# Attention of two heads at a time on the two row halves of TensorE, with one 512-column score product per head

## Chip, cores and metric

One NeuronCore of one Trainium2 chip runs a whole network of four layers on 512 tokens in one launch. The metric is the device time of that launch in microseconds: the median of three runs, beside one profiled execution from which all rows below come.

## The reference, cut to what matters

The last layer's mixer is a neighbourhood attention with 16 heads of 64 channels. The 512 latent tokens lie on a grid of 8 rows by 64 columns; a token sees, in all 8 rows, 16 columns around its own, and 256 context tokens beside them. One softmax runs over both kinds of keys:

```python
s_loc = jnp.einsum('bhrqd,bhrikd->bhrqik', qg, kg).astype(jnp.float32) * scale + bias
s_loc = jnp.where(col_mask[:, None, :], s_loc, NEG_INF)
s_ctx = jnp.einsum('bhrqd,bhcd->bhrqc', qg, k_c).astype(jnp.float32) * scale
s = jnp.concatenate([s_loc.reshape(B_, H, rows, GRID_W, n_loc), s_ctx], axis=-1)
p = jax.nn.softmax(s, axis=-1).astype(v.dtype)
o = jnp.einsum('bhrqik,bhrikd->bhrqd', p_loc, vg) + jnp.einsum('bhrqc,bhcd->bhrqd', p_ctx, v_c)
```

Queries and keys are normalised per head before (`rms_norm_2` with a gain), and the heads' outputs go through `odd_w_o` afterwards. All of it is float32.

## The kernel before, in words

Activations are kept with channels on the 128 partitions and tokens along the free dimension; a number is split in a high and a low part (float32r), and one exact product is three matmuls, high by high, high by low and low by high (`mm3`, L294 to L298). A tile framework puts the instructions of each engine in an order at build time, by priority (which is the order of the program, with some work raised) and by the readiness that its own cost estimates give; on the chip each engine's queue then runs in that order. `load_w` loads a 512 KB weight tile on the SyncE queue, casts its high part on ScalarE and subtracts the low part on VectorE, well ahead of use.

In `odd` the tokens are sorted by grid column, so that 128 queries (16 grid columns, `j` = 0 to 3) need 256 neighbouring keys from `STARTS[j]`. Two heads share one tile of 128 channels: head `hh` = 0 on partitions 0 to 63, `hh` = 1 on 64 to 127. For each pair of heads `hp_` there is a query tile and a key tile `kx` of 704 columns (512 keys and the first 192 again, for the queries at the edge); the context keys are in tiles `kc` of their own. There are 8 x 4 x 2 = 64 items of one head and 128 queries. An item (`item`, L1591) does:

- scores: `mm3` for 256 grid keys and `mm3` for 256 context keys, contraction over 64 rows, into one PSUM tile (L1598, L1599, in the trace under L296 to L298);
- softmax: bias and mask are added and the maximum of the grid half taken in one VectorE instruction (L1602), the maximum of the context half in another (L1604), their joint maximum negated (L1605), two exponentials with sums on ScalarE (L1607, L1608), the sums added, inverted and multiplied in (L1609 to L1611);
- `turn`: four transposes of 128x128 into PSUM (L1617) and a copy to SBUF on ScalarE (L1619);
- `weigh`: four matmuls with the values, whose 64 output rows are the head's half of a PSUM tile `po` (L1625). The two heads of a pair take turns, one key block each.

The loop issues the scores of an item, then a filling piece of other work (`fill`), then the transposes of the item two before and, once more than five items are in the queue, the weighted sums of the two oldest. The filling comes from `side_steps`: the query and key projections of the following pairs of heads, by pieces of two weight blocks (six matmuls of 512 columns), their head norms (`headnorm`, L1426, with one product against `bd64` at L1432), and at the end the first output projections. `fill` stops at a given piece for the last items so that some is left to the end.

Six PSUM tiles (`mm_ps`) serve scores, transposes, projections and head norms alike; two more (`aux_ps`) hold `po`. Ten SBUF tiles (`tmp`) are shared the same way. The bias of a head is loaded per pair (`tb`, L1669) and added to three masks on GpSimd (L1674), with two slots per mask type. Before the loop, the four slots of the probabilities `pr` hold extra key columns `ex` that only the values' products read.

## Time and profile before

| | |
|---|---|
| runs (three) | 2959.49, 2962.75, 2965.26 us; median 2962.75 |
| profiled execution | 2960.36 us, span from first to last instruction 2958.6 us |
| TensorE matmul, busy share | 97% (weight load 82%) |
| VectorE, ScalarE, GpSimd, busy share | 66%, 39%, 21% |
| granted TensorE clock, mean | 0.992 |
| attention loop | about 2317.7 to 2554.1 us of the span |

Busy shares are sums of the instructions' times. Matmuls are pipelined and their printed times overlap, so a matmul's cost in the queue is the distance from its start to the next one's start. "Idle before, releaser" says how long an engine stood before an instruction and which engine ended it. The TensorE instructions of `mm3` all stand under L296 to L298, and are told apart by their tiles: `kh`, `kl`, `kch`, `kcl` with `qh`, `ql` are scores, `hh`, `hl` with `whi`, `wlo` projections.

### The profile page before, as it was taken

The numbers are of one execution on the slowest core, as the hardware profiler recorded it, in microseconds if no ns is written. First come the engines' busy times: TensorE is split into PE (matmuls) and PEld (weight loads), VectorE is DVE, ScalarE is ACT, GpSimd is POOL, SyncE is SP. The second block draws the span as 40 slices with busy tenths as digits, with TensorE's granted clock in tenths as the row PEclk, the third lists the DMA queues.
The fourth block names the chain that finished last, engine by engine and source line by source line (L and its number), as shares of the span: only waits on it lengthen the run. The fifth ranks groups of instructions, "written<-read, shape, count | busy, mean of one in ns | idle before, by whom it ended". The sixth has DMA issues, their size and how long they took to land.

```text
span 2958.6 us, 41163 instructions
## 1 busy us (share of the span) xinstructions
PE 2867.9 (97%) x15892; PEld 2418.0 (82%) x15892; DVE 1960.5 (66%) x3750; ACT 1159.6 (39%) x1993; POOL 614.5 (21%) x568
## 2 busy tenths in 40 slices
PE   5999999999988999999999999999999999999999
PEld 4888888878877887887888888888888777788887
DVE  8767767987877578898636787633366667662333
ACT  4433344323753432323433422222246677542332
POOL 4000003444223113332102122211101122022220
PEclk9999999999999999999999999999999999999999
DMA  7445433665656435554122345412133211133232
GB/s 268 139 154 167 163 108 114 233 211 176 218 191 207 134 114 172 175 182 135 57 77 93 100 135 189 153 62 68 58 97 119 71 47 44 53 98 96 90 106 72
DMA packets 118004, 380.62 MB, mean 129 GB/s; under 512 B 12720, under 2 KB 22576, under 8 KB 116784
## 3 DMA queue, kind: packets, MB, share of 16 engines
q1 hardware_dynamic: 92464, 285.70, 29.6%
q0 software_dynamic: 25344, 92.29, 9.6%
q8 instruction: 125, 2.05, 0.3%
q14 instruction: 71, 0.58, 0.1%
HBM read 354.87 MB, written 23.07 MB: 128 GB/s over the span
## 4 chain that ended last, share of the span: by engine, by line
PE 57%; DVE 8%; ACT 2%; issue 1%; POOL 0%; ACTq 0%; DVEq 0%; POOLq 0%
PE mm L296 18%; PE mm L297 17%; PE mm L298 17%; PE aux L1625 1%; DVE wlo L291 1%; DVE al L280 1%; DVE aout L583 1%; PE mm L1617 1%; DVE araw L583 1%; DVE t L618 1%; ACT whi L290 1%; PE mm L1432 1%; DVE hl L434 0%; ACT ah L279 0%; DVE t L527 0%
## 5 line engine op out<-in xcount | busy, mean ns | idle before, releaser
L296 PE MATMUL mm<-hh,whi 128*128 128x512 f32 (+1 forms) x2872 | 1040.5, 365 | 12.6 <-ACT whi L290 6.0
L297 PE MATMUL mm<-hl,whi 128*128 128x512 f32 (+1 forms) x2872 | 1034.5, 361 | 16.0 <-POOL hl L426 13.6
L298 PE MATMUL mm<-hh,wlo 128*128 128x512 f32 (+1 forms) x2872 | 1033.0, 360 | 0.6 <-DVE wlo L291 0.5
L290 ACT CAST whi<-raw 128x1024 fp32r<-128x1024 f32 (+3 forms) x448 | 447.1, 1002 | 869.4 <-PE mm L297 735.3
L296 PEld LDWEIGHTS mm<-hh,whi 128*128 128x128 f32 x2872 | 543.3, 190 | 102.8 <-ACT whi L290 6.4
L297 PEld LDWEIGHTS mm<-hl,whi 128*128 128x128 f32 x2872 | 546.0, 190 | 98.6 <-POOL hl L426 15.7
L298 PEld LDWEIGHTS mm<-hh,wlo 128*128 128x128 f32 x2872 | 545.7, 190 | 81.7 <-DVE wlo L291 1.3
L291 DVE TENSOR_TENSOR wlo<-raw,whi 128x1024 fp32r<-128x1024 f32 (+4 forms) x316 | 373.4, 1184 | 210.8 <-ACT whi L290 204.5
L291 POOL TENSOR_TENSOR wlo<-raw,whi 128x1024 fp32r<-128x1024 f32 (+3 forms) x132 | 309.6, 2346 | 920.3 <-ACT whi L290 769.9
L297 PE MATMUL mm<-al,whi 128*128 128x512 f32 (+1 forms) x898 | 330.0, 367 | 3.6 <-DVE al L280 3.6
L296 PE MATMUL mm<-ah,whi 128*128 128x512 f32 (+1 forms) x898 | 329.3, 367 | 2.6 <-ACT ah L279 2.6
L298 PE MATMUL mm<-ah,wlo 128*128 128x512 f32 (+1 forms) x898 | 328.9, 366 | 0.0
L583 DVE CUSTOM_DVE_ANT_0 araw<-araw,cond 128x1024 f32<-128x1024 f32 x192 | 249.3, 1299 | 11.3 <-DMA araw<-in_ada 10.8
L618 DVE SCALAR_TENSOR_TENSOR t<-mm,pk,t 128x511 f32<-128x511 f32 (+5 forms) x286 | 161.1, 582 | 134.2 <-ACT t L620 130.8
L579 POOL DMA_DIRECT2D araw<-in_ada x176 | 96.4, 548 | 657.7 <-DVE mod L583 265.5
L297 PEld LDWEIGHTS mm<-al,whi 128*128 128x128 f32 x898 | 170.6, 190 | 31.3 <-DVE al L280 4.6
L296 PEld LDWEIGHTS mm<-ah,whi 128*128 128x128 f32 x898 | 170.6, 190 | 30.4 <-ACT ah L279 3.0
L298 PEld LDWEIGHTS mm<-ah,wlo 128*128 128x128 f32 x898 | 170.5, 190 | 27.3
L710 DVE SCALAR_TENSOR_TENSOR x<-mm,mod,x 128x512 f32<-128x512 f32 (+1 forms) x115 | 84.3, 734 | 141.3 <-PE mm L298 141.1
L643 DVE TENSOR_TENSOR t<-mm,t 128x512 f32<-128x512 f32 x110 | 70.0, 637 | 150.5 <-PE mm L298 112.2
L642 ACT ACTIVATE t<-t 128x512 f32<-128x512 f32 x110 | 64.6, 588 | 268.1 <-DVE t L618 249.6
L280 DVE TENSOR_TENSOR al<-t,ah 128x512 fp32r<-128x512 f32 x110 | 121.8, 1108 | 41.5 <-ACT ah L279 41.3
(368 smaller groups left out, 3619.2 us busy)
## 6 DMA issues: line engine op xcount, KB each, us to landing
araw<-in_ada POOLq DMA_DIRECT2D x176, 512.0 KB, 4.2
raw<-in_up SPq DMA_DIRECT2D x176, 512.0 KB, 3.5
raw<-in_dn SPq DMA_DIRECT2D x32, 448.0 KB, 3.3
raw<-in_dn SPq DMA_DIRECT2D x32, 384.0 KB, 3.1
raw<-in_qk SPq DMA_DIRECT2D x24, 512.0 KB, 3.5
raw<-in_dn SPq DMA_DIRECT2D x32, 320.0 KB, 2.9
araw<-in_ada SPq DMA_DIRECT2D x16, 512.0 KB, 4.6
raw<-in_rqk SPq DMA_DIRECT2D x16, 512.0 KB, 4.4
```

The source lines that it names most:

```text
L280: eng.tensor_tensor(lo, full, hi.bitcast(F32), ALU.subtract)
L290: S.copy(hi[:, :n], raw[:, :n])
L291: next(W["low"]).tensor_tensor(lo[:, :n], raw[:, :n], hi[:, :n].bitcast(F32), ALU.subtract)
L296: T.matmul(o, lhsT=lh[0], rhs=rh[0], start=first, stop=False)
L297: T.matmul(o, lhsT=lh[0], rhs=rh[1], start=False, stop=False)
L298: T.matmul(o, lhsT=lh[1], rhs=rh[0], start=False, stop=last)
L579: (nc.sync if l == 0 and f < 16 else G).dma_start(raw, a[f"ada{l}"][f])
L583: tc.keep_in_program_order(V.tensor_tensor_reduce(out=o, in0=raw, in1=A[c], scale=1.0, scalar=0.0, op0=ALU.mult, op1=ALU.add, accum_out=m))
L618: V.scalar_tensor_tensor(to, fr, cw[q], to, ALU.mult, ALU.add)
L642: S.activation(t, t, AF.Silu)
L643: V.tensor_mul(t, pv, t)
L710: V.scalar_tensor_tensor(xv, p, gates[st.tag][:, f:f + 1], xv, ALU.mult, ALU.add)
```

## The change

The loop goes by pairs of heads, 32 steps instead of 64 items. Context keys are copied by GpSimd behind the grid keys of `kx` (960 columns instead of 704), and a score product takes 256 grid keys and 256 context keys in one matmul of 512 columns with a two-part access pattern. The two heads' matmuls alternate, row half 0 and row half 1, each head into its own PSUM tile: six matmuls a pair instead of twelve. One VectorE instruction per head adds the bias, which is zero over the context columns, negates, and takes the minimum over all 512; one exponential per head with scale -1 follows, then the reciprocal and the scaling. The probabilities now live in the shared `tmp` tiles. A step issues the scores of this pair, the weighted sums of two steps ago, a filling piece, the transposes of the step before, and another filling piece. Bias tiles are allocated once, 512 columns wide; their left half is loaded by DMA and masked in place when the type's last reader of the pair has been issued, so each bias is loaded three times per head. The extra key columns `ex` lie in the slots of two bias types.

```diff
--- before.py
+++ after.py
@@ -1503,7 +1503,7 @@
             V.tensor_scalar(qg, par("qg"), 0.125, None, ALU.mult)
             np2 = stk.enter_context(pool("na2", 2))
             qk = {}
-            ex = [np2.tile([P, 512], F32, tag="pr", name=nm("ex"), bufs=4).bitcast(F32R) for _ in range(4)]
+            ex = [np2.tile([P, 512], F32, tag=f"b{ty}", name=nm("ex")).bitcast(F32R) for ty in (0, 0, 2, 2)]
 
             def ext(k):
                 e = [ex[k // 2][:, (2 * (k % 2) + i) * P:(2 * (k % 2) + i + 1) * P] for i in range(2)]
@@ -1531,14 +1531,17 @@
                     elif step == 9:
                         take(hq, 1)
                     elif step == 15:
-                        kx = (np2.tile([P, 704], F32R, tag="kh", name=nm("kh")), np2.tile([P, 704], F32R, tag="kl", name=nm("kl")))
+                        kx = (np2.tile([P, 960], F32R, tag="kh", name=nm("kh")), np2.tile([P, 960], F32R, tag="kl", name=nm("kl")))
                         hk = headnorm(p, L, par("kg"), kx[0][:, :L], kx[1][:, :L])
+
+                        for i in range(2):
+                            G.tensor_copy(kx[i][:, 704:], kc[hp_][i].bitcast(F32))
                         next(hk)
                     if k % 2:
                         yield
                 take(hk, 1)
-                S.copy(kx[0][:, L:], kx[0][:, :192].bitcast(F32))
-                V.tensor_copy(kx[1][:, L:], kx[1][:, :192].bitcast(F32))
+                S.copy(kx[0][:, L:704], kx[0][:, :192].bitcast(F32))
+                V.tensor_copy(kx[1][:, L:704], kx[1][:, :192].bitcast(F32))
                 qk[hp_] = (q, kx)
 
             os_ = [None] * KT
@@ -1588,51 +1591,58 @@
                 then.h = os_
                 by_halves(then, (5, 6, 7), last_tile, last_add, True)
 
-            def item(hd, j, bias, po):
-                hp_, hh = divmod(hd, 2)
-                rows = slice(64 * hh, 64 * hh + 64)
+            def scores(hp_, j):
+
                 s0 = STARTS[j]
                 q, kx = qk[hp_]
-                p = mm_ps()
-                qs = (q[0][rows, j * P:(j + 1) * P], q[1][rows, j * P:(j + 1) * P])
-                mm3(p[:, :256], qs, (kx[0][rows, s0:s0 + 256], kx[1][rows, s0:s0 + 256]), True, True)
-                mm3(p[:, 256:], qs, (kc[hp_][0][rows, :], kc[hp_][1][rows, :]), True, True)
-                s_ = tmp(256)
-                m = small(4)
-                V.tensor_tensor_reduce(out=s_, in0=p[:, :256], in1=bias[(1, 0, 0, 2)[j]], scale=1.0,
-                                       scalar=NEG, op0=ALU.add, op1=ALU.max, accum_out=m[:, 0:1])
-                V.tensor_reduce(m[:, 1:2], p[:, 256:], mybir.AxisListType.X, ALU.max)
-                V.tensor_scalar(m[:, 0:1], m[:, 0:1], m[:, 1:2], -1.0, ALU.max, ALU.mult)
-                pr = np2.tile([P, 512], F32, tag="pr", name=nm("pr"), bufs=4)
-                S.activation(pr[:, :256], s_, AF.Exp, bias=m[:, 0:1], scale=1.0, accum_out=m[:, 2:3])
-                S.activation(pr[:, 256:], p[:, 256:], AF.Exp, bias=m[:, 0:1], scale=1.0, accum_out=m[:, 3:4])
-                V.tensor_add(m[:, 2:3], m[:, 2:3], m[:, 3:4])
-                V.reciprocal(m[:, 2:3], m[:, 2:3])
-                V.tensor_scalar(pr, pr, m[:, 2:3], None, ALU.mult)
-                pt, prT = [], []
-
-                def turn():
-                    pt.append(mm_ps())
+                ps_ = [mm_ps(), mm_ps()]
+                for qi, ki in ((0, 0), (0, 1), (1, 0)):
+                    for hh in range(2):
+                        rows = slice(64 * hh, 64 * hh + 64)
+                        k_ = kx[ki][rows, s0:s0 + 512]
+                        k_ = dataclasses.replace(k_, ap=[k_.ap[0], [704 - s0, 2], [1, 256]])
+                        T.matmul(ps_[hh].rearrange("p (a b) -> p a b", a=2), lhsT=q[qi][rows, j * P:(j + 1) * P], rhs=k_,
+                                 start=(qi, ki) == (0, 0), stop=qi == 1)
+                prs = []
+                for hh in range(2):
+                    pr = tmp()
+                    m = small(3)
+
+                    V.tensor_tensor_reduce(out=pr, in0=ps_[hh], in1=bias[(1, 0, 0, 2)[j]][hh], scale=-1.0,
+                                           scalar=-NEG, op0=ALU.add, op1=ALU.min, accum_out=m[:, 0:1])
+                    S.activation(pr, pr, AF.Exp, bias=m[:, 0:1], scale=-1.0, accum_out=m[:, 1:2])
+                    V.reciprocal(m[:, 2:3], m[:, 1:2])
+                    V.tensor_scalar(pr, pr, m[:, 2:3], None, ALU.mult)
+                    prs.append(pr)
+                return prs
+
+            def turned(prs):
+                res = []
+                for pr in prs:
+                    p = mm_ps()
                     for b in range(4):
-                        T.transpose(pt[0][:, b * P:(b + 1) * P], pr[:, b * P:(b + 1) * P], ident)
-                    prT.append(tmp())
-                    S.copy(prT[0], pt[0])
-
-                def weigh():
-                    keys = [vt[j][:, hd * 64:(hd + 1) * 64], vt[(j + 1) % 4][:, hd * 64:(hd + 1) * 64]]
-                    keys += [vc[i][hd // 4][:, (hd % 4) * 64:(hd % 4) * 64 + 64] for i in range(2)]
-                    for b in range(4):
-                        T.matmul(po[rows, j * P:(j + 1) * P], lhsT=keys[b],
-                                 rhs=prT[0][:, b * P:(b + 1) * P], start=(b == 0), stop=(b == 3))
-                        yield
-                    if hh == 1 and j == 3:
-                        o = [cpool.tile([P, LC], F32R, tag=f"h{i}c{hp_}", name=nm("o")).bitcast(F32) for i in "hl"]
-                        for i in range(2):
-                            S.copy(o[i], po[:, i * LC:(i + 1) * LC])
-                        ot.append(o)
-                        if hp_ >= 6:
-                            join(hp_)
-                return turn, weigh
+                        T.transpose(p[:, b * P:(b + 1) * P], pr[:, b * P:(b + 1) * P], ident)
+                    res.append(tmp())
+                    S.copy(res[-1], p)
+                return res
+
+            def weigh(hp_, j, prT, po):
+                keys = []
+                for hd in (2 * hp_, 2 * hp_ + 1):
+                    at = slice((hd % 4) * 64, (hd % 4) * 64 + 64)
+                    keys.append([vt[j][:, hd * 64:(hd + 1) * 64], vt[(j + 1) % 4][:, hd * 64:(hd + 1) * 64]]
+                                + [vc[i][hd // 4][:, at] for i in range(2)])
+                for b in range(4):
+                    for hh in range(2):
+                        T.matmul(po[64 * hh:64 * hh + 64, j * P:(j + 1) * P], lhsT=keys[hh][b],
+                                 rhs=prT[hh][:, b * P:(b + 1) * P], start=(b == 0), stop=(b == 3))
+                if j == 3:
+                    o = [cpool.tile([P, LC], F32R, tag=f"h{i}c{hp_}", name=nm("o")).bitcast(F32) for i in "hl"]
+                    for i in range(2):
+                        S.copy(o[i], po[:, i * LC:(i + 1) * LC])
+                    ot.append(o)
+                    if hp_ >= 6:
+                        join(hp_)
 
             ot = []
             side = side_steps()
@@ -1647,51 +1657,39 @@
                     done[0] += 1
                     take(side, 1)
 
-            queue = []
-
-            def advance(t, w):
-
-                n = len(queue)
-                if n > t and not queue[n - 1 - t][2]:
-                    queue[n - 1 - t][0]()
-                    queue[n - 1 - t][2] = True
-                if n > w:
-                    heads = [queue.pop(0)[1]() for _ in range(2)]
-                    for _ in range(5):
-                        for g in heads:
-                            take(g, 1)
-
-            po = None
-            for hp_ in range(8):
-                bias, tb = [{}, {}], []
+
+            bias = [[np2.tile([P, 512], F32, tag=f"b{ty}", name=nm("b")) for _ in range(2)] for ty in range(3)]
+            for ty in range(3):
                 for hh in range(2):
-                    tb_ = np2.tile([P, 256], F32, tag="tb", name=nm("tb"))
-                    nc.sync.dma_start(tb_, a["rpb"][2 * hp_ + hh])
-                    tb.append(tb_)
-                for ty in (1, 0, 2):
-                    for hh in range(2):
-                        b = np2.tile([P, 256], F32, tag=f"b{ty}", name=nm("b"))
-                        G.tensor_tensor(b, tb[hh], msk[:, ty, :], ALU.add)
-                        bias[hh][ty] = b
-                po = aux_ps()
-                for j in range(4):
-                    for hh in range(2):
-                        queue.append([*item(2 * hp_ + hh, j, bias[hh], po), False])
-
-                        fill(72 if hp_ == 7 and j > 1 else 67)
-                        advance(2, 5)
-            while queue:
-                fill(72)
-                for e in queue:
-                    if not e[2]:
-                        e[0]()
-                        e[2] = True
-                        break
-                if queue[1][2]:
-                    heads = [queue.pop(0)[1]() for _ in range(2)]
-                    for _ in range(5):
-                        for g in heads:
-                            take(g, 1)
+                    G.memset(bias[ty][hh][:, 256:], 0.0)
+
+            def biases(hp_, ty):
+                for hh in range(2):
+                    b = bias[ty][hh][:, :256]
+                    nc.sync.dma_start(b, a["rpb"][2 * hp_ + hh])
+                    G.tensor_tensor(b, b, msk[:, ty, :], ALU.add)
+
+            for ty in (1, 0, 2):
+                biases(0, ty)
+            steps = [(hp_, j) for hp_ in range(8) for j in range(4)]
+            prs, prT, pos = {}, {}, {}
+            for n in range(len(steps) + 2):
+
+                upto = 72 if n > 29 else 67
+                if n < len(steps):
+                    hp_, j = steps[n]
+                    if j == 0:
+                        pos[hp_] = aux_ps()
+                    prs[n] = scores(hp_, j)
+                    if hp_ < 7 and j != 1:
+                        biases(hp_ + 1, (1, None, 0, 2)[j])
+                if n > 1:
+                    hp_, j = steps[n - 2]
+                    weigh(hp_, j, prT.pop(n - 2), pos[hp_])
+                fill(upto)
+                if 0 < n <= len(steps):
+                    prT[n - 1] = turned(prs.pop(n - 1))
+                fill(upto)
             take(side, 100)
 
     def dump(name):
```

## Rows read from the trace of the kernel before

**Rows 1.** The loop: us; busy of PE, PEld, DVE, ACT, POOL; clock, DMA share.
```profile
2317.65:2554.10 236.45, 235.64 (x1556) 180.58 (x1555) 162.63 (x540) 162.59 (x441) 50.94 (x56) 1.00 0.13 41
```

**Rows 2.** Chain that ended last, 2326 to 2502 us, by line.
```profile
by line: PE mm L296 29.0%; PE mm L298 19.0%; PE mm L297 18.9%; PE aux L1625 14.6%; PE mm L1617 12.0%; PE mm L1432 6.5%; issue 0.0%
```

**Rows 3.** Waits of PE in the loop: total us, times, longest.
```profile
PE aux L1625 <- ACT t L1619: 0.4, 1, 0.4
PE mm L1432 <- DVE sm L1605: 0.3, 1, 0.3
```

**Rows 4.** PE in order of time, one pair of heads: start, us, instruction.
```profile
2337.66 0.38 PE L296 MATMUL mm<-kh,qh 64*128 64x256 f32 x1
2337.88 0.28 PE L297 MATMUL mm<-kl,qh 64*128 64x256 f32 x1
...
2338.35 0.27 PE L298 MATMUL mm<-kch,ql 64*128 64x256 f32 x1
2338.55 0.50 PE L296 MATMUL mm<-hh,whi 128*128 128x512 f32 x1
2338.89 0.40 PE L297 MATMUL mm<-hl,whi 128*128 128x512 f32 x1
2339.12 0.39 PE L298 MATMUL mm<-hh,wlo 128*128 128x512 f32 x1
...
2340.05 0.60 PE L1617 MATMUL mm<-ident,pr 128*128 128x128 f32 x4
2340.57 0.38 PE L296 MATMUL mm<-kh,qh 64*128 64x256 f32 x1
...
2341.48 0.50 PE L296 MATMUL mm<-hh,whi 128*128 128x512 f32 x1
...
2343.50 0.66 PE L1625 MATMUL aux<-t,vt 128*64 128x128 f32 x8
...
2344.53 0.38 PE L296 MATMUL mm<-kh,qh 64*128 64x256 f32 x1
```

**Rows 5.** PE in order of time elsewhere: one column group, then four in turn.
```profile
525.25 1.95 PE L990 MATMUL aux<-cm,pad 128*32 128x64 f32 x32 [0.46 <-DVE hl L280]
...
864.03 1.08 PE L1083 MATMUL mm<-u,ident 128*32 128x128 f32 x32 [0.79 <-ACT u L1073]
```

**Rows 6.** Groups by line and shape in the loop (L583: page): busy, mean ns.
```profile
L1602 DVE CUSTOM_DVE_ANT_0 t<-mm,b 128x256 f32<-128x256 f32 x64 | 27.1, 423 | 22.0 <-PE mm L298 21.8
L1602 DVE DVE_READ_ACCUMULATOR2_ANT sm<- 128x1 f32 x64 | 5.3, 83 | 0.0
L1604 DVE TENSOR_REDUCE sm<-mm 128x1 f32<-128x256 f32 x64 | 26.8, 419 | 0.0
L1605 DVE TENSOR_SCALAR sm<-sm 128x1 f32<-128x1 f32 x64 | 13.6, 212 | 0.9
L1609 DVE TENSOR_TENSOR sm<-sm 128x1 f32<-128x1 f32 x64 | 11.6, 182 | 19.3 <-ACT pr L1608 19.0
L1607 ACT ACTIVATE pr<-t,sm 128x256 f32<-128x256 f32 x64 | 32.5, 507 | 13.5 <-DVE sm L1605 13.4
L1607 ACT ACTIVATION_READ_ACCUMULATOR pr<-t,sm 128x1 f32 x64 | 12.1, 189 | 0.0
L1608 ACT ACTIVATE pr<-mm,sm 128x256 f32<-128x256 f32 x64 | 29.4, 459 | 0.0
L1619 ACT COPY t<-mm 128x512 f32<-128x512 f32 x64 | 37.1, 581 | 24.8 <-PE mm L1617 24.8
L583 DVE CUSTOM_DVE_ANT_0 araw<-araw,cond 128x1024 f32<-128x1024 f32 x192 | 249.3, 1299 | 11.3 <-DMA araw<-in_ada 10.8
```

**Rows 7.** Order of time, head norm of a key tile: PE, then DVE.
```profile
2389.99 1.13 PE L1432 MATMUL mm<-t,bd 128*128 128x512 f32 x2
...
2394.83 0.74 DVE L1439 SCALAR_TENSOR_TENSOR t<-mm,pk,t 128x512 f32<-128x512 f32 x1
...
2400.41 0.26 DVE L1541 CAST kl<-kl 128x192 fp32r<-128x192 f32 x1 [1.57 <-POOL kl L1442]
```

## Prediction

> **What bounds the kernel now.** I read the busy shares first, then the chain, then the waits, and only then the order of single instructions. Over the attention loop (first score product to last weighted sum, 236.45 us) TensorE is busy 235.64 us, VectorE and ScalarE 162.6 each, GpSimd 50.9, and the granted clock is 1.00 [rows 1]. That share alone could mislead, as matmul times overlap; so the chain: from 2326 to 2502 us every piece of it lies on TensorE, none on a wait [rows 2]. The waits agree: in the whole loop TensorE waited 0.7 us for other engines, twice [rows 3]. So time taken from TensorE's queue here is time taken from the run, until another engine or a latency comes to the surface.
>
> What that queue does is read from start to start, not from the printed times [rows 4]. One head's scores S take 2337.66 to 2338.55, 0.89 us, for six products of 256 columns on 64 rows; the next item's 40.57 to 41.48 is like it, so 0.90. Inside, neighbours start 0.12 apart (37.88 to 38.35 is four starts), so six would take 0.70, and 0.20 is the edge between full-array and half-array products. A second edge follows: the first full product keeps the queue 0.34 (38.55 to 38.89) where the others take 0.23, so 0.11. The filling piece F of six full products is 1.50 (38.55 to 40.05), one head's four transposes T 0.52 (40.05 to 40.57), the weighted sums W of two heads 1.03 (43.50 to 44.53). A pair of heads is two S, two F, two T and one W: 2 x (0.90 + 1.50 + 0.52) + 1.03 = 6.87 us, which is 44.53 - 37.66. There are 32 such pairs.
>
> **Part 1, the score products.** Per pair twelve products of 256 columns become six of 512, alternating between rows 0 to 63 and 64 to 127, into two PSUM tiles. The number of columns is unchanged; what matters is whether the two halves run at once. The trace of before never has two halves of the rows next to each other, so it bounds this only from both sides. One after the other: 6 x 0.23 + 0.20 of edge = 1.58 us. Together: 3 x 0.23 + 0.20 = 0.89. The nearest rows are those of narrow column tiles: 32 instructions of 64 columns, all on one column group, take 1.95 us, while 32 of 128 columns that go round four groups take 1.08 [rows 5]; twice the columns in about half the time, so separate parts of the array do overlap. I take 1.00, a little above the lower end, as six weight loads still pass one by one at the 0.12 spacing seen. Against 2 x 0.90 that saves 0.80, or 0.22 if serial.
>
> Part 3 of the Trainium skill's page "TensorE: Matmul & The Clock Gate" says the same of row halves, but gives 3.07 times for four row groups instead of 4. No run here shows that number; as an estimate by that page, 1.38/(2 x 0.77) + 0.20 = 1.10 us, 3 us less gain over the 32 pairs.
>
> **Part 2, the order of the pieces.** A step now is S, W of two steps ago, F, both T of the step before, F. The edges S to F and T to S occur once instead of twice: the second F follows full-array transposes and costs 6 x 0.23 = 1.38 instead of 1.50. T of two heads in one run is at most 2 x 0.52 = 1.04 and, with one edge of up to 0.20 gone, at least 0.84; I take 0.96. Sum of a step: 1.00 + 1.03 + 1.50 + 0.96 + 1.38 = 5.87 us against 6.87: **1.00 less, 32.0 us over the loop**. With serial halves 6.45, that is 0.42 and 13.4 us.
>
> **Part 3, VectorE and ScalarE.** Removed per pair on VectorE: 2 x (0.423 + 0.083 + 0.419 + 0.212 + 0.182) = 2.64 us; added: two reductions over 512 elements. Those took 0.423 for 256 and 1.299 for 1024 elements, so by a straight line 0.715, plus 0.083: 1.60 [rows 6]. VectorE goes from 162.6/32 = 5.08 to 4.04 us a pair. ScalarE loses two exponentials and two accumulator reads per head (the read behind L1608 priced like that behind L1607), 2 x (0.507 + 0.459 + 2 x 0.189) = 2.69, and gets one of 512 with one read: between 0.581 (a plain copy of 512) and 1.014 (two of 256), I take 0.71 + 0.19; 5.08 - 2.69 + 1.80 = 4.19. Both stay under 5.87, so neither sets the step; over a loop of some 213 us, 129 and 134 us are 61% and 63%, against 69% now.
>
> **Part 4, work moved.** GpSimd gets two copies of 128x256 per pair of head numbers and six memsets at the start, and keeps its six bias additions; 50.9 us of 236 leave room. The SyncE queue issues six bias loads per pair of heads instead of two, each waiting for the reduction that last read that bias; behind them stand weight loads that run tiles ahead, and every bias is due three or four steps later (17 us or more). So nothing on the path; if that cover were gone, a late weight tile would stop F. The bias slots hold the extra columns before the loop (they moved there from the probabilities' slots); the memsets wait for the values' products, which end before the first S, so at most a few tenths. Taken at nothing, up to 3 us.
>
> **Part 5, cover that shrinks.** Three latencies that TensorE now hides get less room.
> (a) Keys of the next pair of heads: the head norm's product starts at 2389.99 and the last copy of the low part ends at 2400.67, 10.7 us [rows 7]. In the new order the distance from that product to the new pair's first S is its own 0.9 (printed as 1.13 with its tail) + 1.50 + 0.96 + 1.38 + a step of 5.87 = 10.6. Before, three items more with one or two W lay between, about 13. So this is level: 0 to 2 us at each of seven boundaries; I take 0.6, 4 us.
> (b) T to W: an item's transposes were three items ahead of its sums (some 10 us); now F and S lie between, 2.4 us, for two copies of 0.581. That leaves 1.2 us for whatever ScalarE is at; I take 0.1 a step, 3 us.
> (c) Two steps near the end (28 and 29) have no F: 1.00 + 1.03 + 0.96 = 3.0 us of TensorE, and 4.0 from the end of S to its T, against a softmax chain of two reductions (1.6), one exponential (0.9) and the reciprocal and scaling behind it. 2 us for the two steps together.
>
> **Sum.** 32.0 - 4 - 3 - 2 = 23 us less. The profiled execution took 2960.36 us (span 2958.6 and 1.8 around it): 2937.4. The median of the runs is 2962.75, 2.4 above it, so on that footing 2939.8; I say **2940**.
>
> **Rivals.**
> Serial halves (the change does not do what it says). For it: no row shows two row halves together, and TensorE takes weights through one queue. Against: rows 5. Then 13.4 less, with fewer waits (say 3): 2952.
> PSUM slots, the slower side. The pool has six tiles: S takes two, the two T take two, the filling holds one, and during a head norm its input and its mean hold two more, seven in all. If S or T has to wait for the head norm to give its input back, TensorE stands from the norm's product at 2389.99 to the end of VectorE's step on that input at 2395.57, 5.6 us, of which the F beside it covers 1.5 [rows 7]; with 14 head norms in the loop that is 14 x 4.1 = 57 us at the worst. The gain of 32 is used up from 2.3 us each; the full price gives 2962.75 - 32 + 57 = 2988, a middling 3.2 us each 2976. The Trainium skill's "TensorEngine Tiling (Array Packing)", Restrictions and Gotchas, speaks for it: row tiles need banks of their own, so row tiling raises the pressure on PSUM. Against: before, up to six were held as well with 0.7 us of waits [rows 3], and scores leave PSUM after the reduction now, not after the exponential.
> Latency takes the gain: (a) and (b) at 0.8 us a step or more, since neither depends on how fast TensorE is. Then 26 of 32 are lost: 2957, no change that shows.
> Two more parts to the better: no stalls at all, 2962.75 - 32 = 2931.
>
> **How the numbers follow.** What a measurement here can tell from no change is 0.2%, 5.9 us: faster is below 2956.8. Forecast, including the better end: 0.68. Serial halves: 0.12. Latency: 0.10, half of it within 0.2%, the rest just under. PSUM: 0.10, mostly slower. Faster 0.68 + 0.11 + 0.03 = 0.82, same 0.09, slower 0.09. The range runs from the better end and a bit for edges that may be cheaper, 2928, to just past the latency case, 2958.
>
> **What would show it.** In the new profile: the six score products of a pair from the first start to the next piece in about 1.0 us (0.9 to 1.1), two starts close together and then 0.23; 1.58 would say serial. A step of 5.9 us in the middle of the loop, waits of TensorE of 5 to 12 us in all, on a key tile, on a copy of transposed probabilities or on a PSUM slot; and a loop of about 213 us in place of 236. VectorE and ScalarE each near 130 to 135 us there. The prediction is wrong if TensorE waits more than 20 us in the loop, if S takes over 1.3 us, or if time moves outside the loop.

## The result: 35.9 us less, and where they came from

The changed kernel takes 2927.59 us (median of 4 runs, 2927.24 to 2928.29), the kernel before, run in turn with it, 2963.44 (4 runs, 2959.49 to 2965.26): 0.9881 of its time, with a 95% interval of 0.9864 to 0.9898. That is 12.4 us below the forecast of 2940 and 0.4 below the low end of the range.

The loop first: from 236.45 us [rows 1] to 203.39, so 33.1 less. The attention starts 1.0 us later and what follows it is 0.6 shorter; the spans differ by 32.7 (2958.6 and 2925.9). The rest of the 35.9 is the choice of executions: the profiled one of before, 2960.36, lies 3.1 us under the median of the runs compared here (2963.44), that of after is like all its runs.

The changed kernel's loop, columns as in [rows 1]:

```profile
2318.67:2522.06 203.39, 202.66 (x1364) 146.76 (x1363) 141.26 (x348) 145.34 (x312) 58.73 (x68) 1.00 0.21 67
```

TensorE is still the bound: busy 202.66 of 203.39 us at a granted clock of 1.00, with 1364 products in place of 1556 (192 fewer: six instead of twelve score products in each of 32 pairs). Its order in the middle of the loop, one step, the counterpart of [rows 4] (start, us, instruction):

```profile
2335.44 0.50 PE L1604 MATMUL mm<-kh,qh 64*128 64x512 f32 x2
2335.77 0.40 PE L1604 MATMUL mm<-kl,qh 64*128 64x512 f32 x2
2336.01 0.40 PE L1604 MATMUL mm<-kh,ql 64*128 64x512 f32 x2
2336.33 0.66 PE L1637 MATMUL aux<-t,vt 128*64 128x128 f32 x8
2336.82 0.61 PE L1637 MATMUL aux<-t,vc 128*64 128x128 f32 x8
2337.36 0.50 PE L296 MATMUL mm<-hh,whi 128*128 128x512 f32 x1
...
2338.87 1.04 PE L1624 MATMUL mm<-ident,t 128*128 128x128 f32 x8
2339.66 0.47 PE L296 MATMUL mm<-hh,whi 128*128 128x512 f32 x1
...
2341.23 0.50 PE L1604 MATMUL mm<-kh,qh 64*128 64x512 f32 x2
```

Read from start to start: S 2335.44 to 2336.33 is 0.89 for both heads (each row is two products, one per half of the rows), W 1.03, F 1.51, T 0.79, F 1.57; the step is 5.79 us where 6.87 stood before. Near the end of the loop the program issues one head's three products alone, and they take 2502.82 to 2503.71, also 0.89:

```profile
2502.82 0.49 PE L1604 MATMUL mm<-kh,qh 64*128 64x512 f32 x1
...
2503.39 0.39 PE L1604 MATMUL mm<-kh,ql 64*128 64x512 f32 x1
2503.71 0.66 PE L1637 MATMUL aux<-t,vt 128*64 128x128 f32 x8
```

So the second head is free in its three products. Charging every interval between two starts to the piece that begins it, the loop is (us; the sums are 2.0 and 1.6 short of the loop, since the last weighted sums have no start behind them):

| piece | before | after | difference | priced |
|---|---|---|---|---|
| S, scores | 57.65 | 34.89 | -22.8 | -25.6 |
| F, filling | 95.68 | 98.10 | +2.4 | -3.8 |
| T, transposes | 34.10 | 26.45 | -7.7 | -2.6 |
| W, weighted sums | 36.57 | 32.45 | -4.1 | 0 |
| N, head norm products | 10.43 | 9.93 | -0.5 | 0 |
| sum | 234.4 | 201.8 | -32.6 | -32.0 |

S is 0.89 to 0.91 in 18 of 32 steps. In 11 others it is 1.09 to 1.35, together 3.6 us over; in three more a filling product stands between the two heads' products, which then cost 0.89 each, 2.7 us. The first kind is a wait for a PSUM slot. TensorE's longest waits in the loop (total us, times, longest), of the matmuls and then of the weight loads ahead of them:

```profile
PE aux L1637 <- ACT t L1626: 0.5, 2, 0.3
```

```profile
PEld mm L1604 <- ACT t L1626: 4.0, 13, 0.4
...
PEld aux L1637 <- ACT t L1626: 1.3, 3, 0.5
```

The first product of the second half waits for ScalarE's copy of a transposed tile, which gives a PSUM slot back. One such place, weight loads and then ScalarE:

```profile
2424.13 0.18 PEld L1604 LDWEIGHTS mm<-kh,qh 64*128 64x128 f32 x1 [0.36 <-issue]
2424.57 0.18 PEld L1604 LDWEIGHTS mm<-kh,qh 64*128 64x128 f32 x1 [0.26 <-ACT t L1626]
```

```profile
2422.03 0.69 ACT L1434 ACTIVATE t<-mm,pk 128x512 f32<-128x512 f32 x1 [0.18 <-PE mm L1432]
...
2423.95 1.05 ACT L1626 COPY t<-mm 128x512 f32<-128x512 f32 x2
```

A head norm's operations stand ahead of the copies on ScalarE, 2422.03 to 2423.95, and the second half starts 0.44 after the first. In ten of the eleven such places a head norm's product lies in the step before.

The merged softmax has nearly the durations that were estimated from the straight line (groups as in [rows 6]):

```profile
L1613 ACT ACTIVATE t<-t,sm 128x512 f32<-128x512 f32 x64 | 45.9, 718 | 32.5 <-DVE sm L1611 32.5
L1611 DVE CUSTOM_DVE_ANT_0 t<-mm,b 128x512 f32<-128x512 f32 x64 | 42.1, 683 | 5.8 <-PE mm L1604 5.6
```

### The profile page after: what moved, and what is told of

Read it like the earlier page. It is cut to its first block, busy times and chain, and to the rows that moved or that the text cites. A ratio compares the mean times of both kernels' runs of the same rounds, so it can differ in the third digit from the quotient of the medians.

```text
span 2925.9 us, 40551 instructions
## 1 busy us (share of the span) xinstructions
PE 2833.4 (97%) x15700; PEld 2382.5 (81%) x15700; DVE 1938.6 (66%) x3558; ACT 1141.8 (39%) x1865; POOL 622.6 (21%) x590
## 4 chain that ended last, share of the span: by engine, by line
PE 55%; DVE 9%; ACT 2%; issue 1%; POOL 0%; ACTq 0%; DVEq 0%; POOLq 0%
PE mm L296 17%; PE mm L297 17%; PE mm L298 17%; DVE aout L583 1%; DVE wlo L291 1%; DVE al L280 1%; DVE araw L583 1%; PE aux L1637 1%; PE mm L1604 1%; PE mm L1624 1%; DVE t L618 1%; ACT whi L290 1%; PE mm L1432 0%; DVE hl L434 0%; ACT ah L279 0%
## 5 line engine op out<-in xcount | busy, mean ns | idle before, releaser
L583 DVE CUSTOM_DVE_ANT_0 araw<-araw,cond 128x1024 f32<-128x1024 f32 x192 | 249.0, 1298 | 12.2 <-DMA araw<-in_ada 11.8
L710 DVE SCALAR_TENSOR_TENSOR x<-mm,mod,x 128x512 f32<-128x512 f32 (+1 forms) x115 | 84.2, 733 | 141.4 <-PE mm L298 141.3
```

The source lines that it names most:

```text
L583: tc.keep_in_program_order(V.tensor_tensor_reduce(out=o, in0=raw, in1=A[c], scale=1.0, scalar=0.0, op0=ALU.mult, op1=ALU.add, accum_out=m))
L710: V.scalar_tensor_tensor(xv, p, gates[st.tag][:, f:f + 1], xv, ALU.mult, ALU.add)
```

## The experiments

Each was timed against the kernel before, whose median lay at 2962.5 to 2963.2 each time. The loop is from the first S to the last W of the profiled run.

| run | us (range) | of before, 95% | loop |
|---|---|---|---|
| after | 2927.59 (2927.24 to 2928.29) | 0.9864 to 0.9898 | 203.4 |
| e1_serial_halves | 2929.15 (2924.41 to 2930.75) | 0.9869 to 0.9898 | 201.0 |
| e2_256_columns | 2930.56 (2928.32 to 2932.03) | 0.9875 to 0.9905 | 204.2 |
| e3_two_maxima | 2951.72 (2951.70 to 2952.41) | 0.9948 to 0.9978 | 226.7 |
| e4_seventh_slot | 2925.56 (2924.82 to 2926.62) | 0.9858 to 0.9891 | 200.5 |
| e5_short_cover | 2937.02 (2933.54 to 2938.59) | 0.9901 to 0.9931 | 210.5 |
| e6_old_order | 2923.27 (2921.75 to 2925.25) | 0.9857 to 0.9886 | 197.3 |
| e7_same_half | 2946.58 (2945.65 to 2948.84) | 0.9932 to 0.9965 | 219.9 |
| e8_two_maxima_slot | 2947.40 (2946.07 to 2948.76) | 0.9938 to 0.9967 | 222.3 |
| e9_old_order_two_maxima | 2949.36 (2948.27 to 2951.02) | 0.9940 to 0.9969 | 223.5 |
| e10_old_order_slot | 2924.24 (2922.17 to 2926.40) | 0.9855 to 0.9884 | 197.8 |
| e11_sums_by_head | 2937.56 (2934.62 to 2938.41) | 0.9899 to 0.9932 | 211.3 |
| e12_merged_softmax_alone | 2958.32 (2956.25 to 2960.43) | 0.9976 to 0.9995 | 232.2 |

**Do the halves run at once, and because they alternate?**

```diff
-                for qi, ki in ((0, 0), (0, 1), (1, 0)):
-                    for hh in range(2):
+                for hh in range(2):
+                    for qi, ki in ((0, 0), (0, 1), (1, 0)):
```

> The changed kernel, but the three score products of the lower rows are issued before the three of the upper rows; same instructions, same columns. Theory (the two row halves run at the same time): one overlap is left, the third with the fourth product, so S goes from 0.89 to 5 x 0.23 + 0.20 = 1.35 us a pair; 32 x 0.46 = 14.7 us more, about 2942. Rival (the gain is fewer, longer products and the order of the pieces, not the halves): S stays near 0.9, about 2928.

The time did not change, so the loss that was expected from three products of one half behind three of the other is not there. The built order of TensorE's queue is indeed one half and then the other, in 31 of the 32 pairs:

```
L1604 MATMUL mm_20457<-kh_20244,qh_20068 128x512
L1604 MATMUL mm_20457<-kl_20245,qh_20068 128x512
L1604 MATMUL mm_20457<-kh_20244,ql_20069 128x512
L1604 MATMUL mm_20458<-kh_20244,qh_20068 128x512
L1604 MATMUL mm_20458<-kl_20245,qh_20068 128x512
L1604 MATMUL mm_20458<-kh_20244,ql_20069 128x512
```

On the chip they run together all the same. S is 0.90 or 0.91 in 23 of the 32 steps; the row below is a step in which the upper half came 0.44 late for its slot, so that the two can be told apart:

```profile
2345.65 0.50 PE L1604 MATMUL mm<-kh,qh 64*128 64x512 f32 x1
2345.99 0.39 PE L1604 MATMUL mm<-kl,qh 64*128 64x512 f32 x1
2346.09 0.49 PE L1604 MATMUL mm<-kh,qh 64*128 64x512 f32 x1
2346.22 0.39 PE L1604 MATMUL mm<-kh,ql 64*128 64x512 f32 x1
2346.42 0.39 PE L1604 MATMUL mm<-kl,qh 64*128 64x512 f32 x1
2346.65 0.39 PE L1604 MATMUL mm<-kh,ql 64*128 64x512 f32 x1
```

The upper half's first product (2346.09) starts before the lower half's third (2346.22), which stands ahead of it in the queue. So TensorE's products do not all start in the built order, as the part on the kernel before has it of every engine's queue. The run alone could not say whether the halves overlap or whether products of 64 rows are simply fast; that took the next one.

```diff
-                        rows = slice(64 * hh, 64 * hh + 64)
+                        rows = slice(0, 64)
```

> The changed kernel, but both heads' score products use rows 0 to 63, so the second head's scores repeat the first head's (its output is not the reference's); same number of instructions and columns, nothing else moved. Theory (the halves of the array's rows run at the same time, whatever the order in the queue, as e1 showed): now they can't, S goes from 0.89 to 6 x 0.23 + 0.20 = 1.58 us, 32 x 0.69 = 22 us more, about 2950. Rival (the halves were never what saved time): 2928.

Same products, same columns, all on one half: S becomes 1.59 (2416.09 to 2417.68) and the kernel 19 us slower than the changed one (22 expected).

```profile
2416.09 0.73 PE L1604 MATMUL mm<-kh,qh 64*128 64x512 f32 x2
...
2417.68 0.55 PE L1637 MATMUL aux<-t,vt 128*64 128x128 f32 x6
```

0.89 against 1.59 for the same work, and 0.89 for one head's three products alone: the halves overlap fully. This overlap is not the whole gain, as the kernel without it still stands 15.9 us below the kernel before.

The page "TensorE: Matmul & The Clock Gate" of the Trainium skill (Part 3, what overlaps and what doesn't) says that matmuls start and end strictly in order and that only weight loads are taken ahead. By that rule the upper half's first product in the swapped order starts no earlier than the lower half's third, 0.46 after the first, its third at 0.92, and S is 0.92 + 0.23 + 0.20 = 1.35 or more. The trace shows 0.90 and the order of starts above, so here the measurement decides against it.

```diff
-                        k_ = kx[ki][rows, s0:s0 + 512]
...
+                for at, fr in ((0, s0), (256, 704)):
+                    for qi, ki in ((0, 0), (0, 1), (1, 0)):
+                        for hh in range(2):
...
+                            T.matmul(ps_[hh][:, at:at + 256], lhsT=q[qi][rows, j * P:(j + 1) * P],
+                                     rhs=kx[ki][rows, fr:fr + 256], start=(qi, ki) == (0, 0), stop=qi == 1)
```

> The changed kernel, but grid keys and context keys in products of 256 columns of their own, twelve a pair, the halves still alternating. If weight loads pass one by one (two of about 0.11 for each pair of products that runs 0.11): 6 x 0.23 + 0.20 = 1.58 us for S, 32 x 0.69 = 22 us more, about 2950. If the loads of the two halves run side by side like the products: S about 0.9, about 2928, and the 512 columns were worth nothing.

Twelve products of 256 columns also take 0.90 (2339.76 to 2340.66), in six pairs whose starts are 0.12 apart after the first:

```profile
2339.76 0.39 PE L1603 MATMUL mm<-kh,qh 64*128 64x256 f32 x2
2339.99 0.28 PE L1603 MATMUL mm<-kl,qh 64*128 64x256 f32 x2
...
2340.66 0.66 PE L1636 MATMUL aux<-t,vt 128*64 128x128 f32 x8
```

Joining grid and context keys in one product gains nothing on TensorE by itself: loads of different halves do not queue up behind each other, against my reason for taking 1.00 instead of 0.89.

**What is the merged softmax worth?**

```diff
-                    V.tensor_tensor_reduce(out=pr, in0=ps_[hh], in1=bias[(1, 0, 0, 2)[j]][hh], scale=-1.0,
-                                           scalar=-NEG, op0=ALU.add, op1=ALU.min, accum_out=m[:, 0:1])
-                    S.activation(pr, pr, AF.Exp, bias=m[:, 0:1], scale=-1.0, accum_out=m[:, 1:2])
+                    V.tensor_tensor_reduce(out=s_, in0=p[:, :256], in1=bias[(1, 0, 0, 2)[j]][hh][:, :256], scale=1.0,
+                                           scalar=NEG, op0=ALU.add, op1=ALU.max, accum_out=m[:, 0:1])
+                    V.tensor_reduce(m[:, 1:2], p[:, 256:], mybir.AxisListType.X, ALU.max)
...
+                    S.activation(pr[:, :256], s_, AF.Exp, bias=m[:, 0:1], scale=1.0, accum_out=m[:, 3:4])
+                    S.activation(pr[:, 256:], p[:, 256:], AF.Exp, bias=m[:, 0:1], scale=1.0, accum_out=m[:, 4:5])
```

> The changed kernel, but the softmax in its old form: two maxima and two exponentials per head, the exponential of the context half read from PSUM. Theory (VectorE and ScalarE stand off the path): 0 to 3 us more, 2928 to 2931; VectorE and ScalarE 1.1 and 0.9 us a pair more busy. Rival (the merged softmax is what lets the step shrink): 10 us or more, over 2938, with TensorE waiting for transposes or PSUM slots.

24 of the 36 us are lost, where 0 to 3 were expected, although neither engine is full: the loop, and the waits of TensorE and of its weight loads for ScalarE's copies (L1631) and for the exponential that reads PSUM (L1617):

```profile
2316.74:2543.42 226.68, 220.86 (x1364) 153.26 (x1363) 177.52 (x540) 159.92 (x440) 56.00 (x68) 0.98 0.20 60
```

```profile
PE aux L1642 <- ACT t L1631: 5.1, 8, 1.9
```

```profile
PEld aux L1642 <- ACT t L1631: 13.4, 23, 2.4
PEld mm L1604 <- ACT t L1631: 2.2, 6, 0.4
PEld mm L1604 <- ACT t L1617: 1.6, 4, 0.6
```

By pieces against the changed kernel: S 46.91 (+12.0), W 38.47 (+6.0), F 102.26 (+4.2), N 11.20 (+1.3). Some 8 of the 12 us of S are not a wait but the order: the queue is laid out when the program is built, by estimated times, and with the longer softmax filling products stand between the two heads' scores in 12 of the 32 steps, where the changed kernel has 3, so that each head pays 0.89 alone. Some 5 us are the clock. From 2330 to 2333 it was granted at 0.50, the lower of its two levels, after TensorE had stood 1.92 us for a copy:

```profile
2330.00:2333.00 3.00, 2.52 (x17) 1.99 (x17) 2.90 (x11) 1.78 (x4) 0.00 (x0) 0.50 0.41 98
```

There W, N and the F behind them take 2.39, 1.08 and 2.89 us, against 1.02, 0.56 and 1.79 at 1.00. The same happens from 2503.5 to 2507 (0.51), after a wait of 1.41: W and N take 2.38 and 1.71, against 1.02 and 0.96.

Two causes for the rest were told apart by giving the PSUM pool a seventh slot, first in the changed kernel, then here. The slot comes from the other pool: the head norm's mean goes there, and the output tile is taken only at its first W.

```diff
-        pm = mm_ps()[:, :n]
+        pm = (mean or mm_ps)()[:, :n]
...
-                    if j == 0:
-                        pos[hp_] = aux_ps()
...
+                    if j == 0:
+                        pos[hp_] = aux_ps()
                     weigh(hp_, j, prT.pop(n - 2), pos[hp_])
```

> The changed kernel, but the head norm's mean goes into the second aux PSUM tile, and the output tile of a pair is taken when its first weighted sum is issued, so scores, transposes, filling and head norm's input share six tiles that suffice. Theory (the twelve to fourteen S of 1.1 to 1.35 us instead of 0.89 wait for a PSUM slot that a copy of transposes frees): these fall to 0.9, 4 us less, about 2923.5. Rival (they wait for something else, or the copy late on ScalarE then holds up W instead): 2928.

S falls from 34.89 to 31.43 us: the 3.5 us are slot waits of the kind read above. W gives 0.8 back (33.22), as its loads now meet the copies, and the loads of S still do at 8 places. The time falls by 2.0 us, half of what the theory said:

```profile
PEld aux L1637 <- ACT t L1626: 6.2, 16, 0.6
PEld mm L1604 <- ACT t L1626: 2.9, 8, 0.7
```

> The kernel with two maxima and two exponentials (2951.7 us), and the head norm's mean in the aux tile as in the seventh-slot kernel. Theory 1 (the exponential that reads PSUM holds the score slots 2 us longer, and slots are what runs out): most of the 24 us comes back, 2930 to 2938. Theory 2 (the longer softmax itself, with ScalarE in order, makes the copies of the transposes and so W late): 2945 or more.

(e3 with e4's edit.) With the slot, the scores stand together again in all steps but one, yet only 4.3 of the 24 us come back; S is 38.37, W 40.65, F 105.16. What is left is, by the trace, the chain of the old softmax: it ends later, so copies are late for W (TensorE stands 2.8 us for them), and the pieces that are moved about to cover it pay edges, the sums W being split in 14 steps. Theory 1 is not quite gone either: TensorE stands 4.8 us more behind exponentials that read PSUM (L1617), in spite of the further slot. No run prices these causes one by one. A better order was tried against them (e6's edit is below):

> Paired score products and the pieces in an order like before (2923.3 us), with the old softmax of two maxima and two exponentials. Between the transposes of a pair and its sums now lie some 6 us instead of 2.4. Theory (the old softmax cost 24 us in the new order because the copies of the transposes came late for W; with more room that is hidden): at most 6 us more, 2923 to 2929. Rival (the longer softmax costs TensorE time in any order, by held score slots or a full ScalarE): 2938 or more.

Nothing is hidden: 26 us against e6. The largest pieces are two stalls beside head norms, where S with the waits in it takes 5.45 us (at 2329) and 4.80 (at 2497). In the first, the second head's scores wait for a PSUM tile that an exponential of the step before still reads, and this exponential stands behind the head norm's cast on ScalarE. TensorE, then ScalarE:

```profile
2329.32 0.49 PE L1604 MATMUL mm<-kh,qh 64*128 64x512 f32 x1
...
2331.94 0.50 PE L1604 MATMUL mm<-kh,qh 64*128 64x512 f32 x1 [1.67 <-ACT t L1617]
```

```profile
2330.32 0.62 ACT L1441 CAST qh<-t 128x512 fp32r<-128x512 f32 x1 [0.51 <-DVE t L1440]
2330.84 0.50 ACT L1616 ACTIVATE t<-t,sm 128x256 f32<-128x256 f32 x1
...
2331.34 0.45 ACT L1617 ACTIVATE t<-mm,sm 128x256 f32<-128x256 f32 x1
```

Last, the merge alone in the kernel before (same two edits of the softmax and biases; heads and the order of the program untouched):

```diff
-                S.activation(pr[:, :256], s_, AF.Exp, bias=m[:, 0:1], scale=1.0, accum_out=m[:, 2:3])
-                S.activation(pr[:, 256:], p[:, 256:], AF.Exp, bias=m[:, 0:1], scale=1.0, accum_out=m[:, 3:4])
+                S.activation(pr, pr, AF.Exp, bias=m[:, 0:1], scale=-1.0, accum_out=m[:, 3:4])
```

> The kernel before, item by item with its own score products and its queue, and only the softmax changed: one reduction over 512 columns with a zero bias on the context half, one exponential, biases reloaded in place as in the change (probabilities of every second item lie in the shared SBUF tiles). It completes the square of paired products and merged softmax: neither 2963, paired alone 2949 to 2952, both 2923 to 2928. Theory (TensorE sets the end in this loop and its products are as before): 2960 to 2964, no change, though VectorE and ScalarE get some 30 us of room each. Rival (the merged softmax also saves TensorE time by itself, through slots or waits that the trace of before shows as full matmuls): 2950 or less.

4.3 us: 2958.32 is just under the 2960 to 2964 of the theory, and clear of no change (0.9976 to 0.9995). In the loop VectorE and ScalarE are busy 16.3 and 12.5 us less, with TensorE still full:

```profile
2320.66:2552.89 232.23, 231.52 (x1556) 179.29 (x1555) 146.32 (x348) 150.08 (x312) 50.46 (x56) 1.00 0.19 59
```

The time was taken from W, 36.57 to 32.93 us by pieces; the others change by 0.4 in all. In the kernel before, other pieces split the sums of 11 of the 32 pairs; here those of two. So it came with the order that was built, as the waits of TensorE in the loop are 0.7 us in both.

The two parts do not add: pairing without the merge gives 11 us (e3; 14 in e9's order), the merge alone 4, both 36.

**What is the order worth?**

```diff
                 fill(upto)
+                fill(upto)
                 if 0 < n <= len(steps):
                     prT[n - 1] = turned(prs.pop(n - 1))
-                fill(upto)
```

> The changed kernel, but both filling pieces ahead of the transposes: S W F F T, so that only S (0.9 us) lies between the transposes of a pair and its weighted sums, and none between the transposes and the next S. Theory (what the short queue of the new order has left is the copy of transposes, 2.4 us for two copies of 0.58, and the head norm's 1.9 us on ScalarE in 14 of 32 steps): W and S wait, 10 to 20 us more, 2938 to 2948. Rival (the copies always have room): 2928.

9.4 us, just under the theory's 10 to 20. With both F ahead of T, only S lies between T and W, and the loads of W wait for the copies 14.2 us in all; W is 1.50 in 11 steps and 5.7 us dearer in the loop:

```profile
PEld aux L1637 <- ACT t L1626: 14.2, 33, 1.1
```

So the second F behind T is the cover that it was said to be.

```diff
-                if n > 1:
-                    hp_, j = steps[n - 2]
-                    weigh(hp_, j, prT.pop(n - 2), pos[hp_])
                 fill(upto)
                 if 0 < n <= len(steps):
-                    prT[n - 1] = turned(prs.pop(n - 1))
+                    prT[n - 1] = turned(prs[n - 1][:1])
                 fill(upto)
+                if 0 < n <= len(steps):
+                    prT[n - 1] += turned(prs.pop(n - 1)[1:])
+                if n > 1:
+                    hp_, j = steps[n - 2]
+                    weigh(hp_, j, prT.pop(n - 2), pos[hp_])
```

> The changed kernel with its scores and softmax, but its pieces in an order like before: S F T(first head) F T(second head) W. The comparison of the two traces gives the order 7.65 (T) + 4.1 (W) - 2.4 (F) = 9.3 us of the 32.6. Theory (that part is edges between kinds of products, which the order alone sets): 7 to 11 us more, 2935 to 2939. Rival (it came with the paired products, not with the order): 2928.

The theory that the new order is worth some 9 us fell. Paired scores in the kernel before's order of pieces (S, F, T of one head, F, T of the other, W) give the shortest loop of all:

```profile
2318.09:2515.37 197.28, 196.26 (x1364) 145.14 (x1363) 142.64 (x348) 145.66 (x312) 55.14 (x68) 1.00 0.23 69
```

```profile
2409.24 0.49 PE L1604 MATMUL mm<-kh,qh 64*128 64x512 f32 x2
...
2413.43 0.60 PE L1624 MATMUL mm<-ident,t 128*128 128x128 f32 x4
2413.96 0.66 PE L1637 MATMUL aux<-t,vt 128*64 128x128 f32 x8
2414.99 0.51 PE L1604 MATMUL mm<-kh,qh 64*128 64x512 f32 x2
```

A step is 5.75 us here (2409.24 to 2414.99), 5.79 there, so the pieces cost nearly the same. What is gone are the slot waits and split steps: S is 29.68 us in all. That the two copies of transposes no longer fall due together would explain it, but the trace shows only that the waits are absent. Its profiled loop is 6.1 us shorter and its time 4.3 lower than the changed kernel's, but the two intervals against before overlap, so its lead is likely and not settled. With the seventh slot as well:

> Paired score products, merged softmax, the pieces in an order like before, and the head norm's mean in the aux tile. In the old-order run S stood at 0.89 in every step of the middle, so no slot was short there. Theory: nothing left to win in the middle, one S of 1.58 at the start; 0 to 1 us less, 2922 to 2923. Rival (slots still delay something): 2920 or less.

Nothing more: where the order asks for no slot, a slot is worth nothing.

```diff
-                for b in range(4):
-                    for hh in range(2):
+                for hh in range(2):
+                    for b in range(4):
```

> The old-order kernel, but the weighted sums W issue the four key blocks of the first head, then the four of the second, instead of alternating; the two heads write the two column halves. Theory from e1 (TensorE starts matmuls of another part of the array ahead of those queued before them): W stays 1.02 us, 2923. Rival (matmuls start in the order of the queue, so halves that don't alternate don't overlap): W about 1.7 us, 32 x 0.7 = 22 us more, 2945.

(On e6.) W goes to halves of the columns, and here the order in the queue does matter: 1.51 instead of 1.02 us, 14 us in all, between the two theories. Each key block stands as two products in the trace. Four products of one half pass alone, then four of each alternate, then four alone:

```profile
2418.60 0.65 PE L1637 MATMUL aux<-t,vt 128*64 128x128 f32 x4
2419.09 0.27 PE L1637 MATMUL aux<-t,vc 128*64 128x128 f32 x1
2419.10 0.32 PE L1637 MATMUL aux<-t,vt 128*64 128x128 f32 x1
...
2419.59 0.60 PE L1637 MATMUL aux<-t,vc 128*64 128x128 f32 x4
2420.12 0.50 PE L1604 MATMUL mm<-kh,qh 64*128 64x512 f32 x2
```

The second head's first product stands eight places behind the first head's first and starts while three of those have not begun; in e1 it stood three behind and started with it.

## Why the prediction was right, and what was mis-sized

**The mechanism held.** TensorE was the bound and stayed it; the gain is TensorE's, in the loop; S went to 0.89 (0.9 to 1.1 was named), the step to 5.79 (5.9), waits of TensorE to 0.7 on the engine (0.5 above and one of 0.2) and 5.3 on its weight loads (5 to 12). Serial halves are refuted by e7.

**Part 1** was 0.11 a step too dear, 3.5 us: the reason given, six weight loads one by one, does not hold between halves (e2). The Trainium skill's 3.07 times, which as an estimate made S 1.10, does not carry over to two halves: here the second costs nothing.

**Part 2** had the sum right by two errors. T was to be 0.96 and the F behind it 1.38; they are 0.79 and 1.57, together 2.36 against 2.34: the edge is there, charged to F. W came out 4.1 us cheaper, which had no term: before, the sums of 11 of the 32 pairs were split by another piece (46 runs of W in the trace) and [rows 4] shows one that was not. The merge alone, with the items as before, gives 3.6 as well (e12), so this part needed neither the pairing nor the new order. And e6 shows that the saved edges of the new order were no gain: the old one needs a step just as long.

**Part 3** priced the operations well (683 against 715 ns, 718 against 710) but not the engines: 141.3 and 145.3 us busy, not 129 and 134. The groups of VectorE's loop do fall by 33.3 us as priced, 188.9 to 155.6 in sum; its busy time falls by 21.4, since neighbours' printed times overlap and busy time counts the overlap once (it is not the sum of the instructions' times, as the part on the profile before has it). Subtracting mean durations from a busy time was the slip. "Neither sets the step" holds, but it hid what the merge is for: with the old softmax two thirds of the gain are lost (e3, e9), with both engines at 71 to 78% of the loop.

**Part 5 is the step that failed:** 9 us for three latencies. (a), the keys (4 us): no wait on a key tile appears. (b), T to W (3 us): 0.5 and 1.3 us. (c), the steps without F (2 us): no wait there either, but two of the three split steps, by the built order, 1.8 us of their 2.7. What was there instead was the PSUM rival in small, 3.6 us of slot waits, not 57: scores give their slot back after the reduction, and what was late was the copy of transposes behind a head norm on ScalarE. A seventh slot takes 3.5 us of such waits off S and 2.0 off the time (e4). The Trainium skill's "TensorEngine Tiling (Array Packing)", Restrictions and Gotchas, was right on the pressure; its price here is those 3.6 us.

In sum: the pieces without stalls gave 39 us rather than 32 (S 3.5, W 4.1, N 0.5, F and T together -1.2), stalls took 6.3 rather than 9, and the 2.4 us that were added for the median were not there after.

**Open.** How the 24 to 26 us of the old softmax divide between late copies, held PSUM tiles, the built order and the lower clock was read from traces (e3: some 8 us order, 5 us clock), but no run separates them, since each moves the others.

## What to carry to other kernels

Put independent products of half the rows next to each other and both halves cost what one does, alternating or three and three; for halves of the columns alternate them. Price such a change together with the engine that follows: two thirds of what the shorter TensorE step gave were lost when the softmax behind it was not shortened too, so a part that is worth little alone may be what lets the others through. And count PSUM slots at each place where pieces ask for them, head norms included: another order of the pieces (e6) did here all that a further slot did (e4).

## What the runs showed of the hardware

- Products on the upper half of the rows, queued behind three on the lower, start with or between them (e1: S 0.90); on one half they take 1.59 (e7).
- Weight loads of the two halves do not add up: twelve products of 256 columns take the 0.90 of six with 512 (e2).
- Products on column halves, eight in a row each, overlap only in the middle: W takes 1.51 against 1.02 when they alternate (e11).
